# Rotated query columns of all heads as two blocks ahead of attention, plain columns by pairs of heads

## The chip, the cores and the metric

The kernel runs on one core of a Trainium2 chip. The metric is the device time of one execution in microseconds, the median of several runs.

## The reference

The program is an encoder of two layers, 1024 positions by 1024 columns, in float32. What the change touches is the query side of the attention branch: a query of a head has 64 plain columns and 32 that are rotated by the position (two halves of 16, x1 and x2).

```python
def apply_rope(x, cos, sin):
    half = x.shape[-1] // 2
    x1, x2 = x[..., :half], x[..., half:]
    return jnp.concatenate([x1 * cos - x2 * sin, x1 * sin + x2 * cos], axis=-1)

def mla_branch(cq, ckv, kr, cos, sin, q_norm_g, w_uq, kv_norm_g, w_ukv, w_oa):
    q = (rmsnorm(cq, q_norm_g) @ w_uq).reshape(B, S, 8, 96)         # 64 plain, 32 rotated
    q_rope = apply_rope(q[..., 64:], cos[:, :, None], sin[:, :, None])
    kv = (rmsnorm(ckv, kv_norm_g) @ w_ukv).reshape(B, S, 8, 128)
    k_nope, v = kv[..., :64], kv[..., 64:]
    k_rope = apply_rope(kr, cos, sin)                               # one for all heads
    q = concatenate([q[..., :64], q_rope]) * 96 ** -0.5
    k = concatenate([k_nope, broadcast(k_rope)])
    ... softmax(q @ k.T) @ v for each head ...
    return o @ w_oa

def reference(...):
    for l in range(2):
        h = rmsnorm(x) * (1 + sc1) + sh1
        cq, ckv, kr, pu, cx, cb, cc, gl = split(h @ w_in[l])
        ya, yb, yc = mla_branch(...), pool_branch(...), conv_branch(...)
        gates = sigmoid(gl + b_gate[l])
        x = x + g1 * ((gates[0] * ya + gates[1] * yb + gates[2] * yc) @ w_out[l])
        x = x + g2 * ec_moe(h2, ...)
    return rmsnorm(x)
```

## The kernel before

Every product of float32 operands is made from a high and a low part: `split` (L115) writes the high part by a cast on ScalarE and the low part by a subtraction on VectorE, and `mm3` (L325) issues three matmuls for each 512 columns: high by high, high by low, low by high. Activations lie with the columns on the partitions and the 1024 positions along the row.

A layer first makes the branches' inputs. From L651 the low-rank query input `cq` (three groups of 128 rows, `cqhi`, `cqlo`) and the key and value input `ckhi`, `cklo` are made and normed. Then a loop of four weight blocks, `for dp in range(4)` (L754), makes the eight parts d = 0 to 7 of the first gate: `proj` (48 matmuls of 128x512 into one `ps` accumulator of 128x1024), a sigmoid on ScalarE (L769), a store of the gate and, on the way, a load, a multiplication (L766) and a store of a part of `w_out`. The weight blocks come through a ring of two buffers each for `raw`, `whi` and `wlo`; three `ps` accumulators rotate. I call this the gate loop.

Attention follows (L779). `v_tile` makes the values. `k_pair` (L805) makes the plain key rows of two heads in one go, 12 matmuls, and splits the query weights of the pair into `qw`: seven pieces, as columns are put in another order: for an even head the 64 plain columns, the 32 rotated ones and once more the 32 with the halves exchanged; for an odd head the other way round. Both heads of a pair so have 128 rows. `q_head` (L826) makes the 128 query rows of one head in two `pa` banks of 512 positions, nine matmuls each; VectorE multiplies a bank by a table (`tab_e` for even heads, `tab_o` for odd: ones in the plain rows, cosine and signed sine in the others) and the result is split into `qs[h]`. The key rows that stand against the rotated ones hold the rotated key `krope` twice (`rope_part`), once for either product, so the scores' sum over 128 rows adds the two.

The work of attention is a list of 64 units (head h, tile t of 128 positions): `scores` (6 matmuls, maximum, exponential, scaling), `trans` (8 transposes through two `pa` banks, split) and, for every second unit, `av` (16 matmul steps with two forms). Scores run two units ahead (LA = 2). Into this order the blocks are put by hand: `q_head(h + 1)` at t = 2 of an even head, `k_pair` of the next pair at t = 1 of an odd head, and `q_head(h + 1)` at t = 4 of an odd head. There are four `pa` banks and two `ps` accumulators in attention. All instructions of an engine run in the order in which they are issued; loads go by SP's queue, stores and a few loads by POOL's.

Of the kernel before, what the change touches and what calls it, by code (L numbers as in the profile page):

```python
# [18 lines left out]
S = 1024  # L19
# [35 lines left out]
def encoder(ctx, tc, x, c, positions, w_mod, b_mod, norm1_g, w_in, b_gate, q_norm_g, w_uq, kv_norm_g,  # L55
# [31 lines left out]
    def ps2():  # L87
        return pstate["pool"].tile([128, 1024], F32, name="ps", tag="ps", bufs=pstate["n"][0])
# [25 lines left out]
    def split(hi, lo, src):  # L114
        return ACT.copy(hi, src), DVE.tensor_sub(lo, src, f(hi))  # L115
# [19 lines left out]
    tabd = dram.tile([2, 128, S], F32, name="tabd")  # L135
# [12 lines left out]
    for q in range(4):  # L148
        for r in range(4):
            DVE.tensor_copy(krsel[32 * r:32 * r + 32, 32 * q:32 * q + 32], ident[0:32, 0:32])  # L150
# [112 lines left out]
    def rope_tables(ip):  # L263
# [29 lines left out]
        one = ip.tile([128, S], F32, name="one", tag="ra")  # L293
        ACT.activation(sn, sn, AF.Copy, scale=sgn)
        DVE.memset(one, 1.0)
        for (i, r, src) in ((0, 0, one), (0, 64, cs), (0, 96, sn), (1, 0, cs), (1, 32, sn), (1, 64, one)):
            n = 64 if src is one else 32
            SP.dma_start(tabd[i, r:r + n, :], src[r:r + n, :])
# [28 lines left out]
    for l in range(DEPTH):  # L327
# [327 lines left out]
        tab_e = Cq.tile([128, S], F32, name="tab_e")  # L655
        SP.dma_start(tab_e, tabd[0])
        tab_o = Cq.tile([128, S], F32, name="tab_o")
        SP.dma_start(tab_o, tabd[1])
        kwhi = Cq.tile([128, 2, 512], F32R, name="kwhi")
        kwlo = Cq.tile([128, 2, 512], F32R, name="kwlo")  # L660
        with pool("cqt", side="left") as cp:
            def low(w, c0):
                p = ps2()
                proj(p, w, c0)
                return p
# [47 lines left out]
            DVE.tensor_mul(kt_[0:64], p[0:64], tab_o[0:64])  # L713
            DVE.tensor_mul(kt_[64:128], p[64:128], tab_e[64:128])
# [12 lines left out]
            split(kwhi, kwlo, raw.rearrange("p k h c -> p k (h c)"))  # L727
            def prepare(pp):
# [24 lines left out]
            for dp in range(4):  # L753
                wg = block()  # L754
                for d in (2 * dp, 2 * dp + 1):
# [22 lines left out]
        with pool("att", side="right") as ap:  # L778
# [27 lines left out]
            def k_pair(hp):  # L806
# [3 lines left out]
                qw[hp] = [ap.tile([128, 3, 256], F32R, name=f"qw{i}", bufs=1) for i in range(2)]  # L810
# [9 lines left out]
                for (d0, s0, n) in ((0, 0, 96), (96, 80, 16), (112, 64, 16),  # L820
                                    (128, 160, 32), (160, 176, 16), (176, 160, 16), (192, 96, 64)):
                    split(qw[hp][0][:, :, d0:d0 + n], qw[hp][1][:, :, d0:d0 + n], raw[:, :, s0:s0 + n])

            def q_head(h):
                w = qw[h // 2]
                i = h % 2  # L826
                cc = slice(128 * i, 128 * i + 128)
                tab = tab_e if i == 0 else tab_o
# [68 lines left out]
            q_head(0)  # L897
# [6 lines left out]
            for n, (h, t) in enumerate(units):  # L904
# [12 lines left out]
                if h % 2 == 0 and t == 2:  # L917
                    q_head(h + 1)
# [643 lines left out]
```

## Time and profile before

| what | value |
|---|---|
| median of 3 runs (lowest, highest) | 3388.4 us (3385.19, 3395.47) |
| the profiled execution: its time, its span | 3388.24 us, 3386.5 us |
| TensorE busy, share of the span | 3201.4 us, 95% |
| VectorE busy | 2442.3 us, 72% |
| ScalarE busy | 1857.7 us, 55% |
| mean granted clock of TensorE | 0.971 |

The profile is one execution of the program. A time in it is in microseconds from the start of the span; its lines name the kernel's line, the engine, the operation and the tiles as out<-in. PE is TensorE, DVE VectorE, ACT ScalarE, POOL GpSimd and SP the engine whose queue issues the loads. In layer 1 the gate loop ends at about 620 us, and attention runs to about 890; layer 2 repeats both some 1670 us later. An idle time in brackets stands with what ended it.

### The profile page before, as it was taken

The numbers are of one execution on the slowest core, as the hardware profiler recorded it, in microseconds if no ns is written. First come the engines' busy times: TensorE is split into PE (matmuls) and PEld (weight loads), VectorE is DVE, ScalarE is ACT, GpSimd is POOL, SyncE is SP. The second block draws the span as 40 slices with busy tenths as digits, with TensorE's granted clock in tenths as the row PEclk, the third lists the DMA queues.
The fourth block names the chain that finished last, engine by engine and source line by source line (L and its number), as shares of the span: only waits on it lengthen the run. The fifth ranks groups of instructions, "written<-read, shape, count | busy, mean of one in ns | idle before, by whom it ended". The sixth has DMA issues, their size and how long they took to land.

```text
span 3386.5 us, 43057 instructions
## 1 busy us (share of the span) xinstructions
PE 3201.4 (95%) x16593; PEld 2672.0 (79%) x16593; DVE 2442.3 (72%) x3730; ACT 1857.7 (55%) x2535; POOL 384.2 (11%) x364
## 2 busy tenths in 40 slices
PE   6999999999978899999989999999998969999996
PEld 5888887788877688888778888887887968888875
DVE  5556525599848899999864355338997489999997
ACT  5111213588634788887631121317885448888876
POOL 2001001000034001001020000010001330001010
PEclk8999999999988899999999999999999979999998
DMA  6346334000445899999622444340015559999994
GB/s 222 118 151 203 125 114 162 33 17 13 138 177 217 301 390 381 388 391 373 254 60 81 132 157 149 103 156 17 20 38 171 199 193 358 387 389 380 389 378 176
DMA packets 283374, 686.00 MB, mean 203 GB/s; under 512 B 24935, under 2 KB 139841, under 8 KB 283169
## 3 DMA queue, kind: packets, MB, share of 16 engines
q1 hardware_dynamic: 247008, 563.13, 44.8%
q0 software_dynamic: 33856, 111.74, 10.4%
q10 hardware_dynamic: 2304, 8.39, 0.7%
q8 instruction: 130, 2.13, 0.3%
q14 instruction: 76, 0.61, 0.1%
HBM read 607.63 MB, written 75.55 MB: 202 GB/s over the span
## 4 chain that ended last, share of the span: by engine, by line
PE 77%; DVE 12%; ACT 4%; DMA 3%; issue 2%; POOL 1%; SPq 0%; POOLq 0%; DVEq 0%; ACTq 0%
PE ps L325 62%; PE pa L1142 4%; DVE wlo L115 3%; PE pa L325 2%; DVE mx L846 2%; PE pa L864 2%; PE ps L1351 1%; PE pa L872 1%; PE pa L874 1%; DMA gh<-gate 1%; ACT pexp L851 1%; ACT whi L115 1%; DVE af L1065 1%; PE pa L1183 1%; DVE top L1063 1%
## 5 line engine op out<-in xcount | busy, mean ns | idle before, releaser
L115 DVE TENSOR_TENSOR wlo<-rg,whi 128x1024 fp32r<-128x1024 f32 x768 | 899.5, 1219 | 99.2 <-ACT whi L115 95.7
L115 ACT CAST whi<-rg 128x1024 fp32r<-128x1024 f32 x768 | 763.8, 1048 | 181.0 <-PE ps L325 181.0
L325 PE MATMUL ps<-whi,T 128*128 128x512 f32 x3072 | 841.8, 393 | 4.0 <-ACT T L115 2.2
L325 PEld LDWEIGHTS ps<-whi,T 128*128 128x128 f32 x3072 | 574.8, 189 | 126.4 <-ACT T L115 3.1
L325 PE MATMUL ps<-wlo,T 128*128 128x512 f32 x1536 | 489.1, 400 | 5.0 <-DVE wlo L115 3.0
L325 PE MATMUL ps<-hhi,whi 128*128 128x512 f32 x1376 | 427.4, 392 | 0.0
L325 PE MATMUL ps<-hlo,whi 128*128 128x512 f32 x1376 | 423.9, 389 | 0.0
L325 PE MATMUL ps<-hhi,wlo 128*128 128x512 f32 x1376 | 423.8, 389 | 0.0
L325 PEld LDWEIGHTS ps<-wlo,T 128*128 128x128 f32 x1536 | 281.3, 189 | 74.3 <-DVE wlo L115 19.0
L115 ACT CAST whi<-raw 128x2048 fp32r<-128x2048 f32 (+2 forms) x59 | 101.1, 1713 | 417.1 <-PE ps L325 360.8
L325 PEld LDWEIGHTS ps<-hhi,whi 128*128 128x128 f32 x1376 | 256.9, 188 | 58.9 <-issue 4.2
L325 PEld LDWEIGHTS ps<-hlo,whi 128*128 128x128 f32 x1376 | 258.3, 188 | 54.1
L325 PEld LDWEIGHTS ps<-hhi,wlo 128*128 128x128 f32 x1376 | 258.3, 188 | 54.0
L1142 PE MATMUL pa<-rg 128*128 128x256 f32 x768 | 191.4, 304 | 28.1 <-DVE rg L115 13.4
L115 DVE TENSOR_TENSOR wlo<-raw,whi 128x2048 fp32r<-128x2048 f32 (+2 forms) x59 | 120.9, 2050 | 98.5 <-ACT whi L115 98.5
L1142 PEld LDWEIGHTS pa<-rg 128*128 128x128 f32 x768 | 148.9, 206 | 31.3 <-DVE rg L115 14.5
L325 PE MATMUL ps<-khi,raw 128*128 128x512 f32 x512 | 166.5, 406 | 7.2 <-ACT pexp L851 5.7
L115 DVE TENSOR_TENSOR wlo<-pa,whi 128x512 fp32r<-128x512 f32 x256 | 169.3, 680 | 1.3 <-ACT whi L115 1.1
L1444 POOL DMA_INDIRECT xres<-y,idx x30 | 72.5, 2416 | 779.4 <-DVE y L1443 779.4
L851 ACT ACTIVATE pexp<-ps,nm 128x1024 f32<-128x1024 f32 x128 | 143.1, 1118 | 30.4 <-DVE nm L848 27.9
L846 DVE TENSOR_REDUCE mx<-ps 128x1 f32<-128x1024 f32 x128 | 155.0, 1212 | 5.4 <-PE ps L325 4.5
L115 ACT CAST whi<-pa 128x512 fp32r<-128x512 f32 x256 | 139.6, 588 | 7.6 <-PE pa L864 6.5
(409 smaller groups left out, 4899.6 us busy)
## 6 DMA issues: line engine op xcount, KB each, us to landing
rg<-in_w_gate_dram SPq DMA_DIRECT2D x128, 1024.0 KB, 8.9
rg<-in_w_up_dram SPq DMA_DIRECT2D x128, 1024.0 KB, 6.9
rg<-in_w_down_dram SPq DMA_DIRECT2D x128, 1024.0 KB, 7.8
raw<-in_w_mod_dram SPq DMA_DIRECT2D x48, 1024.0 KB, 5.4
raw<-in_w_in_dram SPq DMA_DIRECT2D x43, 1024.0 KB, 5.2
part<-pr POOLq DMA_DIRECT2D x32, 512.0 KB, 4.9
pr<-part POOLq DMA_DIRECT2D x16, 512.0 KB, 4.3
sq<-in_w_out_dram POOLq DMA_DIRECT2D x16, 512.0 KB, 4.4
```

The lines of the kernel that those rows point to most:

```text
L115: return ACT.copy(hi, src), DVE.tensor_sub(lo, src, f(hi))
L325: PE.matmul(dst[:, s], a, b[:, s], start=start and i == 0, stop=stop and i == 2)
L846: DVE.reduce_max(mx, p, axis=AX.X)
L851: ACT.activation(e, p, AF.Exp, bias=nm, scale=SCALE, accum_out=sm)
L864: PE.transpose(p[:, 128 * k:128 * k + 128], e[:, o:o + 128], ident)
L872: PE.matmul(po[:, o:o + 256], vt[:, k, h, :], phi[:, k, :], start=(k == 0), stop=False, skip_group_check=True)
L874: PE.matmul(po[0:64, o:o + 256], vt[:, k, h, 0:64], plo[:, k, :], start=False, stop=(k == 7), skip_group_check=True)
L1063: DVE.max(v[:, 15 - r, :], a)
L1065: DVE.match_replace(a, v[:, 15 - r, :], a, -1.0)
L1142: PE.matmul(p[q // 2][:, 256 * (q % 2):256 * (q % 2) + 256], a, wos[q][b][:, k, :], skip_group_check=True, start=(k == 0 and i == 0 and q ...
L1183: PE.matmul(pls[t][:, :E], hT[:, 128 * k:128 * k + 128], wra[:, kk, :], start=(kk == 0), stop=(kk == 7))
L1444: POOL.indirect_dma_start(out=xres[l], in_=y, in_offset=None, compute_op=OP.add, out_offset=bass.IndirectOffsetOnAxis(ap=idx[e][:, 0:1], a ...
```

## The change

`q_head` goes, and with it the tables `tab_e`, `tab_o` and the doubled columns. In its place:

- `q_rope`, once a layer, in the gate loop behind the gate's part d = 3 (its weights are asked for at d = 2). The rotated columns of all eight heads are two blocks of 128 columns: x1 of all heads, x2 of all heads. Each is 18 matmuls of 128x512 into one `ps` accumulator. Cosine and sine are loaded; four multiplications, a subtraction and an addition of 128x1024 rotate all heads at once; both results are split, and high and low parts stored to memory (`qrd`) in four stores of 512 KB.
- `q_pair`, four times a layer: the 64 plain columns of two heads stand together in one block of 128, 18 matmuls into two `pa` banks. Each bank is split by halves, 64 rows to the one head's query tile and 64 to the other's. The rotated rows come by two loads of 256 KB a head from `qrd`, on SP's queue. The second copy meets key rows that are zero now (`krsel`, which spreads the rotated key over the rows, is filled for two of four groups).
- The query weights of a pair are split in one piece. Every third head's queries have a tile of their own (`q3`).
- `q_pair` stands at t = 4 of an odd head and ahead of the first unit; at the even heads nothing is put in.
- The tables in memory are cosine, sine, and one for the key.

```diff
+            def q_rope(raw):
+                w = [W.tile([128, 3, 2, 8, 16], F32R, name=n_, tag=n_) for n_ in ("whi", "wlo")]
+                for i in range(2):
+                    split(w[0][:, :, i], w[1][:, :, i], raw[:, :, :, 16 * i:16 * i + 16])
...
+                for i in range(2):
+                    p = ps2()
+                    for k in range(3):
+                        mm3(p, w[0][:, k, i], w[1][:, k, i], cqhi[:, k], cqlo[:, k], k == 0, k == 2)
+                    ps.append(p)
...
+                SP.dma_start(cos, tabd[0])
+                SP.dma_start(sin, tabd[1])
...
+                for i, (a, b) in enumerate(((cos, sin), (sin, cos))):
+                    DVE.tensor_mul(r[2 * i], ps[0], a)
+                    DVE.tensor_mul(r[1], ps[1], b)
+                    (DVE.tensor_add if i else DVE.tensor_sub)(r[2 * i], r[2 * i], r[1])
+                    lo = r[2 * i].bitcast(F32R)
+                    split(hi, lo, r[2 * i])
+                    POOL.dma_start(qrd[l][i, :, 0, :], f(hi))
+                    POOL.dma_start(qrd[l][i, :, 1, :], r[2 * i])
...
                     POOL.dma_start(gate0d[l][d], g)
+                    if d == 2:
+                        rope_raw = q_rope_load()
+                    if d == 3:
+                        q_rope(rope_raw)
...
-                for (d0, s0, n) in ((0, 0, 96), (96, 80, 16), (112, 64, 16),
-                                    (128, 160, 32), (160, 176, 16), (176, 160, 16), (192, 96, 64)):
-                    split(qw[hp][0][:, :, d0:d0 + n], qw[hp][1][:, :, d0:d0 + n], raw[:, :, s0:s0 + n])
-
-            def q_head(h):
...
-                qs[h] = W.tile([128, 2, S], F32R, name="raw", tag="raw", bufs=2)
+                split(qw[hp][0], qw[hp][1], raw.rearrange("p k (i c) -> p k i c", c=96)[:, :, :, 0:64])
+
+            def q_pair(hp):
+
+                w = [a.rearrange("p k i c -> p k (i c)") for a in qw[hp]]
+                for h in (2 * hp, 2 * hp + 1):
+                    if h % 3 == 2:
+                        qs[h] = ap.tile([128, 2, S], F32R, name="q3", bufs=1)
+                    else:
+                        qs[h] = W.tile([128, 2, S], F32R, name="raw", tag="raw", bufs=2)
+                    r = 64 * (1 - h % 2)
+                    for o in (0, 32):
+                        SP.dma_start(f(qs[h][r + o:r + o + 32]), qrd[l][:, 16 * h:16 * h + 16])
                 for q in range(2):
                     s_ = slice(512 * q, 512 * q + 512)
                     p = ps1()
                     for k in range(3):
-                        mm3(p, w[0][:, k, cc], w[1][:, k, cc], cqhi[:, k, s_], cqlo[:, k, s_], k == 0, k == 2)
-                    qf = ap.tile([128, 512], F32, name="pexp", tag="pexp", bufs=3)
-                    DVE.tensor_mul(qf, p, tab[:, s_])
-                    split(qs[h][:, 0, s_], qs[h][:, 1, s_], qf)
+                        mm3(p, w[0][:, k], w[1][:, k], cqhi[:, k, s_], cqlo[:, k, s_], k == 0, k == 2)
+                    for i in range(2):
+                        r = slice(64 * i, 64 * i + 64)
+                        split(qs[2 * hp + i][r, 0, s_], qs[2 * hp + i][r, 1, s_], p[r])
...
-                    q_head(h + 1)
                     if h + 1 == H - 1:
...
                     if t == 4:
-                        q_head(h + 1)
+                        q_pair(h // 2 + 1)
```

Where the rope block stands on TensorE, in the middle of the gate loop of layer 1 (`hhi`, `hlo` are the gate's input, `cqhi`, `cqlo` the query input; `wrs` is a small step behind one of the gate's parts). Before, behind the sixth part:

```order
L325 MATMUL ps<-hlo,whi 128x512 x2
L325 MATMUL ps<-hhi,wlo 128x512 x2
L750 MATMUL pa<-wrs,ones 128x16
L325 MATMUL ps<-hhi,whi 128x512 x2
L325 MATMUL ps<-hlo,whi 128x512 x2
```

Now, behind the fourth:

```order
L328 MATMUL ps<-hhi,whi 128x512 x2
L328 MATMUL ps<-hlo,whi 128x512 x2
L328 MATMUL ps<-hhi,wlo 128x512 x2
L784 MATMUL pa<-wrs,ones 128x16
L328 MATMUL ps<-cqhi,whi 128x512 x2
L328 MATMUL ps<-cqlo,whi 128x512 x2
L328 MATMUL ps<-cqhi,wlo 128x512 x2
```

The small step has moved two parts forward, and the 18 groups of the rope block (36 matmuls) stand behind it, ahead of the fifth part.

ScalarE in the same place, with the semaphores that each row waits for (`cf<-ps,vec` is a sigmoid of the gate, `whi<-raw` a cast of weights). Before:

```order
L769 ACTIVATE cf<-ps,vec 128x1024 [waits PE_49]
L115 CAST ckhi<-cf 128x1024 [waits DVE_49] x2
L115 CAST whi<-raw 128x2048 [waits DMAHW6_49,PE_49]
L769 ACTIVATE cf<-ps,vec 128x1024 [waits DMASW5_49,PE_49,Activation_49]
L769 ACTIVATE cf<-ps,vec 128x1024 [waits DVE_49,PE_49]
L115 CAST whi<-raw 128x2048 [waits DMAHW7_49,PE_49]
```

Now:

```order
L115 CAST whi<-raw 128x2048 [waits DMAHW5_49,PE_49]
L803 ACTIVATE cf<-ps,vec 128x1024 [waits DMASW5_49,PE_49,Activation_49]
L803 ACTIVATE cf<-ps,vec 128x1024 [waits DVE_49,PE_49]
L115 CAST whi<-raw 128x3x128 [waits DMAHW6_49,DMAHW7_49,DMAHW0_49,PE_49]
L115 CAST whi<-raw 128x3x128
L803 ACTIVATE cf<-ps,vec 128x1024 [waits DVE_49,PE_49]
L115 CAST whi<-raw 128x2048 [waits DMAHW1_49,DVE_49,PE_49]
L115 CAST rhi<-cf 128x1024 [waits DMASW2_49,DMASW6_49,DMASW1_49,DVE_49]
L115 CAST rhi<-cf 128x1024 [waits DMASW3_49,DVE_49,Activation_49]
L803 ACTIVATE cf<-ps,vec 128x1024 [waits DMASW7_49,PE_49]
```

Two casts of rope weights have come in ahead of the next weight block's cast, and wait for TensorE; the casts of the rotated rows (`rhi`) stand between a weight block and the next sigmoid.

VectorE in attention, in the second half of head 1, where the queries of head 2 were made and those of heads 2 and 3 are made now (`wlo<-pa` is the split behind a transpose, `mx` and `nm` belong to the scores). Before:

```order
L884 TENSOR_TENSOR op<-pa,otmp 64x512
L836 TENSOR_TENSOR pexp<-pa,tab_e 128x512
L115 TENSOR_TENSOR raw<-pexp,raw 128x512
L836 TENSOR_TENSOR pexp<-pa,tab_e 128x512
L846 TENSOR_REDUCE mx<-ps 128x1
L115 TENSOR_TENSOR raw<-pexp,raw 128x512
L848 TENSOR_SCALAR nm<-mx 128x1
```

Now:

```order
L925 TENSOR_TENSOR op<-pa,otmp 64x512
L115 TENSOR_TENSOR q_4922<-pa,q_4922 64x512
L115 TENSOR_TENSOR raw<-pa,raw 64x512
L115 TENSOR_TENSOR qw_5497<-uq,qw_5496 128x384
L115 TENSOR_TENSOR q_4922<-pa,q_4922 64x512
L887 TENSOR_REDUCE mx<-ps 128x1
L115 TENSOR_TENSOR raw<-pa,raw 64x512
L889 TENSOR_SCALAR nm<-mx 128x1
L115 TENSOR_TENSOR wlo<-pa,whi 128x4x128 x2
```

Two multiplications and two subtractions of 128 rows have become four subtractions of 64 rows, which read the accumulator `pa` themselves; the subtraction of query weights in one piece stands between them. The like rows of the even heads, four of them with seven pieces of query weights, have nothing in their place.

## Rows read from the trace of the kernel before

**Rows 1.** The page, parts 1 and 4: busy time by engine, chain by engine.

```profile
PE 3201.4 (95%) x16593; PEld 2672.0 (79%) x16593; DVE 2442.3 (72%) x3730; ACT 1857.7 (55%) x2535; POOL 384.2 (11%) x364
...
PE 77%; DVE 12%; ACT 4%; DMA 3%; issue 2%; POOL 1%; SPq 0%; POOLq 0%; DVEq 0%; ACTq 0%
```

**Rows 2.** Table by stretches: gate loop, a pair of heads (columns: first line).

```profile
core 0: us, PE busy (x) PEld busy (x) DVE busy (x) ACT busy (x) POOL busy (x), PEclk, DMA share, GB/s
560.00:620.00 60.00, 60.00 (x267) 49.73 (x266) 12.35 (x14) 8.34 (x7) 9.57 (x18) 1.00 0.47 167
665.88:729.48 63.60, 63.16 (x402) 55.09 (x400) 59.38 (x120) 53.61 (x99) 0.53 (x1) 1.00 0.04 14
```

**Rows 3.** Timeline of TensorE, gate loop: start, duration (us), line, operation.

```profile
571.77 0.62 PE L325 MATMUL ps<-hlo,whi 128*128 128x512 f32 x2
...
576.75 0.61 PE L325 MATMUL ps<-hhi,whi 128*128 128x512 f32 x2
...
581.74 0.62 PE L325 MATMUL ps<-hhi,wlo 128*128 128x512 f32 x2
```

**Rows 4.** Timeline of TensorE in attention, a query block and two units.

```profile
761.14 0.39 PE L325 MATMUL pa<-cqhi,qw 128*128 128x512 f32 x1
...
765.27 0.61 PE L325 MATMUL ps<-khi,raw 128*128 128x512 f32 x2
...
771.63 0.63 PE L325 MATMUL ps<-khi,raw 128*128 128x512 f32 x2
...
778.03 0.63 PE L325 MATMUL ps<-khi,raw 128*128 128x512 f32 x2
```

**Rows 5.** VectorE's groups in one pair: busy us, mean ns, idle before.

```profile
L115 DVE TENSOR_TENSOR wlo<-pa,whi 128x512 fp32r<-128x512 f32 x33 | 21.8, 681 | 0.0
...
L836 DVE TENSOR_TENSOR pexp<-pa,tab_e 128x512 f32<-128x512 f32 x2 | 1.4, 692 | 0.1
...
L115 DVE TENSOR_TENSOR qw<-uq,qw 128x48 fp32r<-128x48 f32 x4 | 0.6, 200 | 0.0
L115 DVE TENSOR_TENSOR qw<-uq,qw 128x288 fp32r<-128x288 f32 x1 | 0.4, 448 | 0.0
L115 DVE TENSOR_TENSOR qw<-uq,qw 128x192 fp32r<-128x192 f32 x1 | 0.4, 351 | 0.0
L115 DVE TENSOR_TENSOR qw<-uq,qw 128x96 fp32r<-128x96 f32 x1 | 0.3, 251 | 0.0
```

**Rows 6.** Timelines: VectorE and ScalarE in the gate loop, TensorE's wait after it.

```profile
571.73 1.23 DVE L766 TENSOR_TENSOR sq<-sq,rk 128x1024 f32<-128x1024 f32 x1 [6.45 <-DMA sq<-in_w_out_dram]
...
576.50 1.91 ACT L115 CAST whi<-raw 128x2048 fp32r<-128x2048 f32 x1 [9.31 <-PE ps L325]
...
629.06 0.50 PE L325 MATMUL pa<-cqhi,qw 128*128 128x512 f32 x1 [1.39 <-ACT qw L115]
```

**Rows 7.** Timeline of the first key block: ScalarE and VectorE on one half.

```profile
626.35 0.58 ACT L115 CAST khi<-pa 64x512 fp32r<-64x512 f32 x1
...
627.18 0.67 DVE L115 TENSOR_TENSOR klo<-pa,khi 64x512 fp32r<-64x512 f32 x1
```

**Rows 8.** DMA issues from 540 to 640 us: count, KB each, us to landing.

```profile
sq<-in_w_out_dram POOLq DMA_DIRECT2D x8, 512.0 KB, 4.4
...
woutd<-sq POOLq DMA_DIRECT2D x8, 512.0 KB, 3.4
```

**Rows 9.** Table by stretches: around a gap of TensorE in either layer.

```profile
648.00:652.00 4.00, 2.17 (x14) 1.67 (x14) 4.00 (x8) 2.77 (x5) 0.00 (x0) 1.00 0.00 0
652.00:656.00 4.00, 4.00 (x16) 3.30 (x17) 2.93 (x6) 2.45 (x4) 0.00 (x0) 0.57 0.00 0
2318.00:2322.00 4.00, 2.17 (x15) 1.66 (x13) 4.00 (x8) 2.78 (x6) 0.00 (x0) 1.00 0.00 0
2322.00:2326.00 4.00, 4.00 (x29) 3.69 (x30) 4.00 (x11) 3.51 (x6) 0.00 (x0) 1.00 0.00 0
```

More of the change, by code (lines that the diff above doesn't have):

```diff
@@ L134, in encoder @@
     gate0d = [dram.tile([8, 128, S], F32, name=f"gate0{l}") for l in range(DEPTH)]
-    tabd = dram.tile([2, 128, S], F32, name="tabd")
+    tabd = dram.tile([3, 128, S], F32, name="tabd")
+    qrd = [dram.tile([2, 128, 2, S], F32, name=f"qrd{l}") for l in range(DEPTH)]
     woutd = [dram.tile([8, 128, D], F32, name=f"woutd{l}") for l in range(DEPTH)]
@@ L147, in encoder @@
     krsel = consts.tile([128, 128], F32, name="krsel")
-    for q in range(4):
+    DVE.memset(krsel, 0.0)
+    for q in (0, 2):
         for r in range(4):
@@ L292, in rope_tables @@
         DVE.tensor_scalar(sgn, sgn, 0.125, -1.0, op0=OP.mult, op1=OP.add)
[L293 to L298, printed above, removed]
+        turned = ip.tile([128, S], F32, name="turned", tag="ra")
+        ACT.activation(turned, sn, AF.Copy, scale=sgn)
+        SP.dma_start(tabd[0], cs)
+        SP.dma_start(tabd[1], sn)
+        for (r, src) in ((0, cs), (32, turned), (64, cs), (96, turned)):
+            SP.dma_start(tabd[2, r:r + 32, :], src[r:r + 32, :])
     def rms_scale(src, n, scr):
@@ L654, in encoder @@
         krope = Cq.tile([128, S], F32, name="krope")
[L655 to L658, printed above, removed]
         kwhi = Cq.tile([128, 2, 512], F32R, name="kwhi")
@@ L661, in encoder @@
         with pool("cqt", side="left") as cp:
+            tab_k = cp.tile([128, S], F32, name="tab_k")
+            SP.dma_start(tab_k, tabd[2])
             def low(w, c0):
@@ L712, in encoder @@
             kt_ = cp.tile([128, S], F32, name="cf", tag="cf", bufs=3)
-            DVE.tensor_mul(kt_[0:64], p[0:64], tab_o[0:64])
-            DVE.tensor_mul(kt_[64:128], p[64:128], tab_e[64:128])
+            DVE.tensor_mul(kt_, p, tab_k)
             def k_rope():
@@ L727, in encoder, with q_rope_load @@
             split(kwhi, kwlo, raw.rearrange("p k h c -> p k (h c)"))
+            def q_rope_load():
+                raw = W.tile([128, 3, 8, 32], F32, name="raw", tag="raw")
+                for k in range(3):
+                    SP.dma_start(raw[:, k], w_uq[l][128 * k:128 * k + 128, :].rearrange("p (h c) -> p h c", c=96)[:, :, 64:96])
+                return raw
+            def q_rope(raw):
+                w = [W.tile([128, 3, 2, 8, 16], F32R, name=n_, tag=n_) for n_ in ("whi", "wlo")]
+                for i in range(2):
+                    split(w[0][:, :, i], w[1][:, :, i], raw[:, :, :, 16 * i:16 * i + 16])
+                w = [a.rearrange("p k i h c -> p k i (h c)") for a in w]
+                ps = []
+                for i in range(2):
+                    p = ps2()
+                    for k in range(3):
+                        mm3(p, w[0][:, k, i], w[1][:, k, i], cqhi[:, k], cqlo[:, k], k == 0, k == 2)
+                    ps.append(p)
+                cos, sin = (cp.tile([128, S], F32, name="sq", tag=n_, bufs=1) for n_ in ("sq", "rb"))
+                SP.dma_start(cos, tabd[0])
+                SP.dma_start(sin, tabd[1])
+                r = [cp.tile([128, S], F32, name="cf", tag="cf", bufs=3) for _ in range(3)]
+                hi = cp.tile([128, S], F32R, name="rhi")
+                for i, (a, b) in enumerate(((cos, sin), (sin, cos))):
[6 more added lines that the diff above has]
+                    POOL.dma_start(qrd[l][i, :, 1, :], r[2 * i])
             def prepare(pp):
@@ L809, in k_pair @@
                 SP.dma_start(raw, w_uq[l][:, 192 * hp:192 * hp + 192].rearrange("(k p) f -> p k f", p=128))
-                qw[hp] = [ap.tile([128, 3, 256], F32R, name=f"qw{i}", bufs=1) for i in range(2)]
+                qw[hp] = [ap.tile([128, 3, 2, 64], F32R, name=f"qw{i}", bufs=1) for i in range(2)]
                 cc = slice(128 * hp, 128 * hp + 128)
@@ L896, in encoder @@
             k_pair(0)
-            q_head(0)
+            q_pair(0)
             for u in units[:LA]:
```

4 lines of the change are left out of this document (removed).

## Prediction

> **What bounds the kernel now.** I read the page first: its list of busy times and its chain of work that ended last [rows 1]. TensorE is busy 95% of the span, and 77% of the chain is its own work, so an edit is worth what it takes from TensorE or makes it wait. A whole-span average hides stages, so next I read the table by stretches for the two places that the change touches [rows 2]. In the gate loop (560 to 620 us) TensorE is busy all 60.00 us while VectorE has 12.35 and ScalarE 8.34: there a matmul costs its own length, and everything else has room. In attention one pair of heads (665.88 to 729.48) takes 63.60 us, TensorE 63.16, VectorE 59.38, ScalarE 53.61; that is TensorE's bound too, but with VectorE only 4 us behind. The granted clock is 1.00 (its upper level, 2.4 GHz) in both stretches.
>
> Third, the timelines of TensorE, for the price of one matmul at each place. In the gate loop 44 matmuls of 128x512 lie between the starts 571.77 and 581.74 [rows 3]: 9.97 / 44 = 0.2266 us each. In attention a query block's 18 matmuls run from 761.14 to the next scores at 765.27 [rows 4]: 4.13 us. Two units (a unit is one 128-row tile of one head: scores, transposes, half an a·v) run from 771.63 to 778.03: 6.40 us. A pair has 16 units, two query blocks and one key block of 12 matmuls: 8 × 6.40 + 2 × 4.13 + 12 × 0.2266 = 62.2 of the 63.60 us. So some 1.4 us a pair is left for waits, and a block that vanishes should shorten the pair by its whole length.
>
> **What goes.** Query blocks: 8 a layer become 4, so 4 × 2 layers × 4.13 = 33.0 us of TensorE. VectorE loses, per pair, four multiplications with the tables (0.692 us) and seven small subtractions of query weights (0.4 + 0.6 + 0.4 + 0.3) [rows 5] for which one of 128x384 comes; between the pieces of 288 (448 ns) and of 512 columns (681 ns) I estimate it at 0.55 us. That is 2.8 + 1.15 = 3.9 us, so VectorE goes from 59.4 to 55.5 in a pair whose TensorE time goes to 63.60 − 4.13 = 59.5. The ratio of the two stays at 0.93: VectorE does not become the bound, and is no less close to it.
>
> **What comes.** The rope block in the gate loop: 36 matmuls a layer, 36 × 0.2266 = 8.16 us, 16.3 for both layers. Its VectorE work (six operations of 128x1024, 1.23 us each by the 1.23 us of such a multiplication [rows 6], two subtractions for the split, two small ones for weights: about 11 us) lies in a stretch where VectorE is free four fifths of the time, and is free as long as that stays so. The next gate blocks need the accumulators it reads: three pairs of banks rotate there and a gate block takes 48 × 0.2266 = 10.9 us, longer than the two multiplications that read each, so I cost that at nothing.
>
> **The wait ahead of it.** In the order of ScalarE the casts of the rope weights stand directly behind the fourth gate block, and they write the buffer that this block's last matmuls read. Before, at such a place, the cast began at 576.50 [rows 6] while the next block's matmuls began at 576.75 [rows 3]: it starts some 0.25 us ahead of the end, once the last reader of the high part is done. A cast of 512 columns took 0.58 us [rows 7]; by columns 384 would take 0.44, by length alone 0.58, so my estimate is 0.5 us, and TensorE can go on another hand-off later: a wait of about 0.5 us a layer. The ends are 0 (cast hidden behind the two matmuls with the low part) and 1.39 us, which TensorE waited for query weights at 629.06 [rows 6]. I take 0.5, nearest to the row at the same place: 1.0 us for both.
>
> **DMAs and queues.** Per layer there are four more stores of 512 KB on the POOL queue and, on the SP queue, 16 loads of 256 KB, three of rope weights and one table more than before. Stores of 512 KB landed in 3.4 us and loads of 512 KB in 4.4 [rows 8]; DMA was busy 0.47 in the gate stretch and 0.04 in attention [rows 2]. Behind the rope block stand four gate blocks, 43.5 us, ahead of attention's first read; the four stores, with the three transfers of one gate block among them, are some 25 us. In attention a load waits only for the last reader of its tile, at least seven units (22 us) ahead of its use. Behind them on SP stands nothing due sooner than the next pair's weights, and on POOL the gate stores that nobody reads until the merge. I cost all this at nothing; with that cover gone, one late load is its 4.4 us.
>
> **The new query block.** Two heads share one bank now. ScalarE's cast of one half, VectorE's subtraction, then the second half's cast and subtraction go strictly one behind the other, since each row waits for the other engine's. Before, a bank was free after one multiplication of 0.69 us. At the key block, which has the same half-bank form, the cast started at 626.35, the subtraction at 627.18, and it lasted 0.67 [rows 7]: 1.50 us for one half, 3.0 for a bank. The first bank's chain ends 0.94 us after the block's last matmul (3.0 less the 2.06 that the second bank's nine matmuls take), the second's 3.0 later, at 3.94. Scores use other banks, 1.36 us for six matmuls; one bank of the four is free for the first transposes; the first of the two comes free before the second transposes, and the second (3.94 us) before the next unit's (3.20 + 1.36). Counted by this TensorE needn't wait. Other work in the two queues will stretch it: I allow 0.7 us, half of the 1.4 us a pair loses now, and the block that vanished gives the same back. Net 0, between −0.7 (nothing waits) and +3.9 us a pair (TensorE stands until the last half is out).
>
> By the Trainium skill, PSUM — Partial Sum Buffer, "PSUM bank collisions raise a hardware error", two engines need keeping apart only in the same bank and the same quadrant of 32 partitions. The two halves are in different quadrants, so the alternation is stricter than the page asks, and with both in parallel a bank would be free sooner than my 3.0 us; the order of the changed kernel keeps it, so the sum stays as it is. By the page alone a bank would need 0.58 + 1.50 = 2.1 us, and (b) below would be 2.1 × 8 = 17, about 3389 us; no row here shows two engines in one bank at once.
>
> **The sum**, against the profiled execution of 3388.24 us (the median of the three runs is 3388.4, so nothing shifts): 3388.24 − 33.0 + 16.3 + 1.0 + 0 = **3372.5 us**, 0.46% less. About 0.3% is what a measurement of this kernel can tell from no change: 3378.1 and 3398.4.
>
> **Rivals.** (a) *Each query block costs one half-bank chain.* Place: second transposes behind the block wait 1.5 us, because casts and subtractions of other units stand between the halves. For it: VectorE's 59.38 of 63.60 leaves it little slack; against: the count above. 8 × 1.5 = 12: 3384.5 us. It leaves the forecast's side from 0.7 us a block, (3378.1 − 3372.5) / 8.
>
> (b) *Slower: TensorE stands until the last half is out.* 3.94 × 8 = 31.5: 3404.0 us. It decides from 15.7 / 8 = 1.96 us a pair, and is measurably slower from 3.2. For it: the alternation and two heads in one chain; against: scores don't need these banks, and one bank is free.
>
> (c) *The gap ahead of the rope block lowers the clock.* After 1.83 us without a matmul (TensorE busy 2.17 of 4 us, 648 to 652) the granted clock was 0.57 in the next 4 us; after an equal gap in the second layer (2318 to 2322) it stayed at 1.00 [rows 9]. If the rope block ran wholly at the lower level, its 36 matmuls would cost twice as much, 16.3 us more for both layers: 3388.8 us, no change. Against it: my wait is 0.5 us, not 1.83, and one of two longer gaps left no mark. The Trainium skill, TensorE: Matmul & The Clock Gate, "What's actually happening", says that the gate halves the clock after idleness and restores it with activity; by that rule, a gap of this kind either costs nothing or a short stretch, and these rows agree and show both outcomes.
>
> (d) *It doesn't do what it says*: rotated rows arrive late, or the scheduler's order turns the saved blocks into waits for exponentials. The pair keeps its 63.6 us: TensorE's saving goes and the rope block stays, 3388.24 + 17.3 = 3405.5 in full, or about no change with half of it. I see no row for it.
>
> (e) *Better*: the waits around the vanished block go as well, 0.7 × 8 = 5.6: 3366.9 us.
>
> **How the numbers follow.** Forecast (3371 to 3377, by the hand-off's bounds and small waits) 0.52; (e) 0.07; (a) 0.17, of which 0.03 under 0.7 us a block; (c) 0.09; (b) 0.10; (d) 0.05, with 0.01 of it slower. Faster: 0.52 + 0.07 + 0.03 = 0.62. Within 0.3%: 0.14 + 0.09 + 0.04 = 0.27. Slower: 0.10 + 0.01 = 0.11. The range goes from 3365 (just under (e)) to 3389 (just over (c)), leaving out (b), part of (d) and some of (e).
>
> **What would show it.** In the trace after: a pair of heads at 59.5 us with TensorE some 59 busy (right), or 61 and more with idle time ahead of transposes, put down to VectorE's subtraction on a half bank (a, b). The gate loop longer by 8.2 + 0.5 us a layer, with one idle gap of about half a microsecond, put down to ScalarE's cast, ahead of the first rope matmul; a granted clock below 1.00 behind it means (c). An idle gap put down to a load of query rows means (d). I'm wrong if the pair shortens by less than 3 us, or the rope block costs more than 10 us a layer.

## The result and the profile after

The changed kernel takes 3369.15 us (median of 7 runs, 3365.76 to 3375.81) against 3388.4 us (median of 7, 3383.96 to 3395.47); the ratio is 0.9948, 95% interval 0.9939 to 0.9958. That is 19.2 us less, where 15.7 were forecast (3372.5 us). The profiled execution took 3369.31 us, its span is 3367.5.

The page after, parts 1 and 4, as [rows 1]:

```profile
PE 3182.2 (94%) x16521; PEld 2656.2 (79%) x16521; DVE 2432.3 (72%) x3660; ACT 1853.9 (55%) x2495; POOL 388.7 (12%) x372
...
PE 78%; DVE 11%; issue 3%; ACT 3%; DMA 3%; POOL 1%; SPq 0%; POOLq 0%; ACTq 0%; DVEq 0%
```

TensorE's busy time fell by 19.2 us and VectorE's by 10.0. The table by stretches, as [rows 2] (gate loop, the rope block alone, the second and third pair of heads):

```profile
560.00:620.00 60.00, 59.98 (x266) 49.59 (x265) 22.44 (x24) 11.28 (x11) 11.30 (x22) 1.00 0.69 236
577.34:585.50 8.16, 8.16 (x36) 6.75 (x37) 2.43 (x4) 1.48 (x3) 0.53 (x1) 1.00 0.70 195
689.78:749.21 59.43, 58.99 (x386) 51.82 (x384) 55.85 (x111) 52.83 (x94) 0.53 (x1) 1.00 0.09 32
749.21:808.61 59.40, 58.96 (x385) 51.81 (x383) 56.13 (x110) 52.52 (x94) 0.53 (x1) 1.00 0.08 32
```

The rope block takes 8.16 us for its 36 matmuls. A pair of heads takes 59.43 and 59.40 us, 4.2 less than before; VectorE is busy 55.85 of them. Both are as forecast. What was not forecast stands between the two places. TensorE's timeline, first query block of layer 1 and of layer 2:

```profile
641.91 0.80 PE L328 MATMUL pa<-cqhi,qw 128*128 128x512 f32 x1 [6.94 <-ACT qw L115]
...
2303.35 0.79 PE L328 MATMUL pa<-cqhi,qw 128*128 128x512 f32 x1 [5.12 <-ACT qw L115]
```

The idle time in brackets is 6.94 and 5.12 us; before it was 1.39 us there [rows 6] (1.58 in layer 2). To see where time came and went I cut each layer at the starts of four matmuls that both kernels have: the first value matmul, the second key block, the fourth key block, and the first matmul of the merge behind attention. Differences after less before, in us:

| stretch | forecast | layer 1 | layer 2 |
|---|---|---|---|
| up to the first value matmul (gate loop with the rope block; for layer 2 from the first layer's merge) | +8.7 | +7.2 | +7.2 |
| first value matmul to second key block (entry of attention) | −4.1 | −1.4 | −1.4 |
| second to fourth key block (two pairs) | −8.3 | −8.4 | −8.4 |
| fourth key block to the merge | −4.1 | −4.0 | −5.1 |
| sum | −7.9 | −6.6 | −7.7 |

That is −14.3 of the span's −19.0. The other 4.7 us lie behind layer 2's merge, in code that the change doesn't touch: 827.96 us before, 823.26 after. In the eleven experiments below the same stretch took between 824.7 and 827.4 us, in kernels of either kind, so executions differ there by some 3 us of themselves; the two values compared here lie just outside this range, one at either end. Whether a part of the 4.7 belongs to the change stays open.

### The profile page after: what moved, and what is told of

It reads as the page before. It is cut to its first block, busy times and chain, and to the rows that moved or that the text cites. A ratio compares the mean times of both kernels' runs of the same rounds, so it can differ in the third digit from the quotient of the medians.

```text
span 3367.5 us, 42973 instructions
## 1 busy us (share of the span) xinstructions
PE 3182.2 (94%) x16521; PEld 2656.2 (79%) x16521; DVE 2432.3 (72%) x3660; ACT 1853.9 (55%) x2495; POOL 388.7 (12%) x372
## 4 chain that ended last, share of the span: by engine, by line
PE 78%; DVE 11%; issue 3%; ACT 3%; DMA 3%; POOL 1%; SPq 0%; POOLq 0%; ACTq 0%; DVEq 0%
PE ps L328 63%; PE pa L1182 4%; PE pa L905 3%; DVE wlo L115 3%; PE pa L913 2%; PE pa L915 2%; PE pa L328 1%; PE ps L1391 1%; DMA gh<-gate 1%; ACT whi L115 1%; DVE af L1105 1%; DVE gh L1014 1%; DVE top L1103 1%; DVE mx L887 1%; PE ps L493 1%
## 5 line engine op out<-in xcount | busy, mean ns | idle before, releaser
L115 ACT CAST whi<-raw 128x2048 fp32r<-128x2048 f32 (+3 forms) x63 | 103.0, 1637 | 429.9 <-PE ps L328 382.9
L115 DVE TENSOR_TENSOR wlo<-raw,whi 128x2048 fp32r<-128x2048 f32 (+3 forms) x63 | 123.0, 1955 | 97.0 <-ACT whi L115 96.9
L232 DVE SCALAR_TENSOR_TENSOR macc<-raw,csil,macc 128x256 f32<-128x256 f32 x280 | 135.1, 484 | 8.4
```

Of the source, the lines that this page charges most:

```text
L232: DVE.scalar_tensor_tensor(acc, raw[:, k], csil[:, k:k + 1], acc, op0=OP.mult, op1=OP.add)
```

## The entry of attention: where a forecast gain went

Why does TensorE stand there? The timelines of SP, POOL and ScalarE in the changed kernel, layer 1:

```profile
629.36 1.25 SPq L870 DMA_DIRECT2D q<-qrd  x2
...
630.83 0.53 POOL L804 DMA_DIRECT2D gate<-cf  x1 [10.40 <-ACT cf L803]
...
639.30 1.07 ACT L115 CAST vt<-pa 128x512 fp32r<-128x512 f32 x2 [7.69 <-issue]
640.26 1.07 ACT L115 CAST khi<-pa 64x512 fp32r<-64x512 f32 x2
641.35 0.51 ACT L115 CAST qw<-uq 128x384 fp32r<-128x384 f32 x1
...
2300.73 1.07 ACT L115 CAST vt<-pa 128x512 fp32r<-128x512 f32 x2 [5.87 <-DMA gate<-cf]
```

Read from below: the cast of the first query weights (641.35) stands on ScalarE behind the keys' cast and the first value split (639.30). That split waited 7.69 us; the profile names no releaser in layer 1, but in layer 2 (the last row) it names the store of the last gate. The value tile lies where the last gates' tiles were, so it has to wait for their stores. The last store was issued at 630.83, 8.5 us before the split started and 1.5 us behind two loads of rotated rows (629.36) on the other queue. The DMA lists from 600 to 645 us (count, KB each, median us to landing), of the kernel before and of the changed one, and the changed one's table by stretches read:

```profile
gate<-cf POOLq DMA_DIRECT2D x3, 512.0 KB, 2.9
...
gate<-cf POOLq DMA_DIRECT2D x4, 512.0 KB, 8.8
...
625.00:630.00 5.00, 5.00 (x24) 4.14 (x23) 0.00 (x0) 0.58 (x1) 0.00 (x0) 1.00 0.13 55
635.00:640.00 5.00, 0.00 (x0) 0.00 (x0) 0.08 (x1) 0.70 (x2) 0.00 (x0) 0.88 0.13 53
640.00:645.00 5.00, 3.09 (x7) 2.49 (x8) 4.54 (x7) 4.90 (x9) 0.00 (x0) 0.50 0.28 96
...
2300.00:2305.00 5.00, 1.65 (x4) 1.36 (x5) 3.65 (x6) 4.22 (x7) 0.00 (x0) 0.61 0.13 54
2305.00:2310.00 5.00, 5.00 (x17) 3.93 (x17) 2.87 (x5) 3.39 (x6) 0.00 (x0) 0.71 0.30 99
```

A gate store that landed in 2.9 us now takes 8.8. While only loads of rotated rows run (625 to 630, 635 to 640) the DMA share is 0.13, the share of two of sixteen engines, and 53 to 55 GB/s move: 256 KB then take almost 5 us. If a store is spread over all sixteen engines, it ends only when its part on those two does; the traces don't show single engines, so this is argued. My theory A: the loads run on two engines, the last gate store waits behind them there, the value split waits for the store, the query weights for the split, TensorE for the weights. Rivals: theory B, that the volume of transfers or ScalarE's own order makes the wait, whatever the loads' form; and, for the sum as a whole, that the gain in a pair came from VectorE's and ScalarE's lost work and not from TensorE's.

The Trainium skill, DMA: Bandwidth & Descriptors, "Rules for kernel authors", says that a transfer whose outermost dimension has a size c below 16 stays on at most c DMA engines. The loads read from two blocks (x1 and x2) of 16 rows, so c is 2; the share of 0.13 agrees.

The clock shows a second price. After the idle time the granted clock was 0.50 in layer 1 (640 to 645), the lower of its two levels, and 0.61 and 0.71 in layer 2. The 18 matmuls of the query block and the 12 of two scores cost 6.84 us at the upper level (18 × 0.229 + 12 × 0.2266); they took 8.7 and 9.1 us, from 641.91 to the next value matmul at 650.60 and from 2303.35 to 2312.43.

## The experiments

Each run was taken beside runs of the kernel before, whose median was 3386.2 to 3386.8 us in these sets and 3388.4 us in the first. So a difference of medians of two sets is uncertain by some 2 us from this alone; for smaller differences I go by the stretches of the trace.

**The loads spread wide.** Theory A's first link.

```diff
                     for o in (0, 32):
-                        SP.dma_start(f(qs[h][r + o:r + o + 32]), qrd[l][:, 16 * h:16 * h + 16])
+                        for i in range(2):
+                            SP.dma_start(f(qs[h][r + o + 16 * i:r + o + 16 * i + 16]), qrd[l][i, 16 * h:16 * h + 16])
```

> The changed kernel with each head's rotated rows loaded by four loads of 128 KB (16 rows of 8 KB each) in place of two of 256 KB (two times 16 rows); same bytes, same queue, same places. Theory A: in the changed kernel the loads of 256 KB keep only two of the sixteen DMA engines busy (DMA share 0.13 while they run), the last gate store is held up on those two, the first value split on ScalarE waits for that store, and TensorE stands 6.94 and 5.12 us ahead of the first query block with its clock down after it. Spread wider, the wait falls to 1 to 2 us in each layer and the granted clock stays near 1.00 behind it: 12 to 16 us less, about 3355 us. Theory B: the number of DMA engines is not what matters (the volume of transfers or ScalarE's own order is): the two waits stay, 3369 us as the changed kernel.

Measured: 3361.97 us (ratio to before 0.9928, 0.9914 to 0.9941). TensorE's first query block in both layers, then the gate stores and the loads in the DMA list from 585 to 645 us, then the table by stretches:

```profile
637.67 0.50 PE L328 MATMUL pa<-cqhi,qw 128*128 128x512 f32 x1 [3.08 <-ACT qw L115]
...
2294.56 0.79 PE L328 MATMUL pa<-cqhi,qw 128*128 128x512 f32 x1 [2.86 <-ACT qw L115]
...
gate<-cf POOLq DMA_DIRECT2D x4, 512.0 KB, 5.8
...
raw<-qrd SPq DMA_DIRECT2D x8, 128.0 KB, 5.2
...
q<-qrd SPq DMA_DIRECT2D x4, 128.0 KB, 4.2
...
600.00:605.00 5.00, 5.00 (x24) 4.14 (x23) 0.00 (x0) 0.00 (x0) 1.08 (x3) 1.00 1.01 389
625.00:630.00 5.00, 5.00 (x24) 4.05 (x22) 0.00 (x0) 0.97 (x1) 0.00 (x0) 1.00 0.05 8
...
2295.00:2300.00 5.00, 5.00 (x13) 3.83 (x13) 3.00 (x5) 3.95 (x6) 0.00 (x0) 0.50 0.43 111
```

The idle time fell from 6.94 and 5.12 to 3.08 and 2.86 us. The same bytes now go at full rate (share 1.01 and 389 GB/s where they run beside the stores), and those of heads 0 and 1 are over before the last gate block ends (0.05 from 625 to 630). The value split started 4.6 us behind the last gate store's issue (630.43 to 635.05), not 8.5. The entry took 4.0 us less in layer 1, but only 1.6 in layer 2: there the clock fell after the shorter gap too (0.50 from 2295 to 2300, last row), and the 30 matmuls of the query block and two scores took 9.72 us (2294.56 to 2304.28) where they took 9.08 in the changed kernel. Theory A holds for the loads' form; my number was too high, since a wait of 3 us stays and the clock didn't stay up: 7.2 us by the medians, and 5.6 when each kernel is set against the kernel before of its own set, which is also the sum of the two entries; not 12 to 16.

The form isn't all of the stores' delay: with the same bytes in wide loads a gate store still lands in 5.8 us (first row of the DMA list), between the 2.9 before and the 8.8 of the changed kernel, so the volume of transfers, theory B's part, has a share in it. Nor did the edit change the form alone: two of head 2's four loads went out behind the store, at 639.08, so that half as many of head 2's bytes stood ahead of it. The next run takes all of them from there.

**Head 2's loads behind the store.** The order of the two transfers.

```diff
-                        SP.dma_start(f(qs[h][r + o:r + o + 32]), qrd[l][:, 16 * h:16 * h + 16])
+                        (POOL if h == 2 else SP).dma_start(f(qs[h][r + o:r + o + 32]), qrd[l][:, 16 * h:16 * h + 16])
```

> The changed kernel with the two loads for head 2 alone issued on POOL's queue, so that they stand behind the last gate store and not ahead of it; all other loads as they are. Theory A (the store is held up by the loads issued just ahead of it): the store lands 3 to 4 us after its issue, the wait of TensorE falls to about 2 us in each layer, 8 to 14 us less, about 3358 us. If the loads of heads 0 and 1 still held the store up, the wait would stay at 5 us or more. Theory B (volume or order on ScalarE): 3369 us.

Measured: 3365.37 us (0.9935, 0.9922 to 0.9949). Timeline of TensorE:

```profile
637.52 0.80 PE L328 MATMUL pa<-cqhi,qw 128*128 128x512 f32 x1 [4.22 <-ACT qw L115]
...
2296.77 0.79 PE L328 MATMUL pa<-cqhi,qw 128*128 128x512 f32 x1 [4.51 <-ACT qw L115]
```

The idle time is 4.22 and 4.51 us: less than in the changed kernel, more than the 2 us expected, and in layer 2 hardly less. The entry took 2.9 us less in layer 1 and in layer 2 as long as before the edit (59.15 us for 59.17). The value split started 5.8 and 6.0 us behind the store's issue, so the store wasn't out 3 to 4 us behind it, as I had expected. Part of my 2 us was too little from the start: even with wide loads the split started 4.6 us behind, with 3.08 us of idle TensorE. What this run has above the idle time with wide loads is 1.1 and 1.7 us; heads 0 and 1 still load in the old form, and head 2's loads now run beside the store. It speaks for A weakly, and in layer 1 alone. It also speaks against fewer bytes ahead of the store as the explanation of what wide loads gained: with none of head 2's ahead of it the wait was longer, not shorter.

**Without the rope block's matmuls**, on narrow loads and on wide ones. What does the block cost?

```diff
-                    p = ps2()
-                    for k in range(3):
-                        mm3(p, w[0][:, k, i], w[1][:, k, i], cqhi[:, k], cqlo[:, k], k == 0, k == 2)
-                    ps.append(p)
...
+                ps = [f(cqhi[:, 0]), f(cqhi[:, 1])]
```

> The changed kernel without the 36 matmuls and the weights of the rope block: the rotation is fed from two groups of the query input, so the rotated columns are not the reference's; all multiplications, splits, stores and loads stay. By the prediction's sum the block is 8.16 us of TensorE in each layer and no wait: 16.3 us less, 3353 us. If the gate loop were set by its transfers or by VectorE now that the rotation stands in it, the time would stay nearer to 3369 us.

> The changed kernel with the loads spread wide (four of 128 KB a head) and without the 36 matmuls and weights of the rope block (rotation fed from the query input, so the rotated columns are not the reference's). Beside the kernel with wide loads alone (3361.97 us) it prices the block where no transfer is late. Theory A (the block costs its 36 matmuls, 8.16 us a layer; the run without it on narrow loads was slower only because the loads then came last): 16 us less, 3346 us, TensorE's wait ahead of the first query block 3 to 6 us. Theory B (transfers behind the rotation are the bound whatever their width): the wait grows by about 8 us a layer and the time stays at 3360 us or more.

Measured on narrow loads: 3380.73 us (0.9983, 0.9973 to 0.9992), 11.6 us more than the changed kernel with 72 matmuls fewer, where I had expected 3353 or, at worst, 3369. On wide loads: 3348.44 us (0.9887, 0.9872 to 0.9902), 13.5 less than with the block. The waits ahead of the first query block, narrow and then wide, with ScalarE's value split of the narrow one:

```profile
644.35 0.80 PE L328 MATMUL pa<-cqhi,qw 128*128 128x512 f32 x1 [16.62 <-ACT qw L115]
...
2311.02 0.80 PE L328 MATMUL pa<-cqhi,qw 128*128 128x512 f32 x1 [20.72 <-ACT qw L115]
...
641.74 1.07 ACT L115 CAST vt<-pa 128x512 fp32r<-128x512 f32 x2 [18.73 <-DMA q<-qrd]
```

```profile
622.45 0.50 PE L328 MATMUL pa<-whi,ckhi 128*128 128x512 f32 x1 [1.21 <-ACT cf L794]
...
631.63 0.50 PE L328 MATMUL pa<-cqhi,qw 128*128 128x512 f32 x1 [3.44 <-ACT qw L115]
...
2281.19 0.80 PE L328 MATMUL pa<-cqhi,qw 128*128 128x512 f32 x1 [4.00 <-ACT qw L115]
```

With narrow loads the time that TensorE no longer spends on the block comes back as waiting, and more: 16.62 and 20.72 us, and the value split waited 18.73 us until the transfers were out. The entry is set by the end of the slow transfers, and the four gate blocks behind the rotation are what hides them; in the changed kernel this cover was too short. The missing 8.16 us of cover, added to the old waits, would make 15.1 and 13.3 us; the 1.5 and 7.4 us above that stay unexplained. With wide loads the block is worth what its matmuls say: 16.3, less 2.4 for a wait that its absence brings back (1.21 us ahead of the first value matmul in each layer, first row of the second fence) and 1.5 for a longer wait ahead of the query block (3.44 and 4.00, not 3.08 and 2.86), leaves 12.4; 13.5 were measured.

**Query matmuls put back**, 18 at each even head, read by nobody.

```diff
                 if h % 2 == 0 and t == 2:
+                    w = [a.rearrange("p k i c -> p k (i c)") for a in qw[h // 2]]
+                    for q in range(2):
+                        s_ = slice(512 * q, 512 * q + 512)
+                        p = ps1()
+                        for k in range(3):
+                            mm3(p, w[0][:, k], w[1][:, k], cqhi[:, k, s_], cqlo[:, k, s_], k == 0, k == 2)
```

> The changed kernel with 18 matmuls put back at the third unit of every even head, into two banks that nobody reads: four such blocks a layer, no work for another engine. If TensorE's own time sets a pair of heads, as the prediction's sum has it, each costs 4.13 us: 33 us more, about 3402 us, and a pair goes back from 59.4 to 63.5 us. If the pair's gain came from VectorE's and ScalarE's work that went with the old blocks, the matmuls fit into waits and the time stays under 3385 us.

Measured: 3401.93 us (1.0042, 1.0028 to 1.0055), 32.8 more than the changed kernel by the medians; the touched stretches of the two traces differ by 31.3. Its second pair in the table by stretches:

```profile
694.25:757.52 63.27, 62.94 (x404) 55.23 (x402) 56.19 (x110) 52.77 (x94) 0.53 (x1) 1.00 0.08 30
```

A pair takes 63.27 us, nearly what it took before (63.60), though VectorE has only 56.19 us of work in it. So 3.9 of the 4.2 us that a pair gained come back with the matmuls alone: the pair's gain is TensorE's time, and the rival falls.

**The first key block ahead of the values**, meant to get the query weights' cast out from behind the value split. On narrow loads, on wide ones, and in the kernel before:

```diff
+            k_pair(0)
             for t in range(2):
                 v_tile(t)
-            k_pair(0)
             q_pair(0)
```

> The changed kernel, loads narrow as they are, with the first key block put ahead of the first two value tiles, and so the casts of keys and query weights ahead of the value split that waits for the last gate store. Theory A (TensorE stands because the casts of query weights are queued on ScalarE behind that split): TensorE works through keys, values and the first query block meanwhile, the idle ahead of the first query block falls from 6.9 and 5.1 to under 1 us, some 2 us may come back ahead of the first scores: 8 to 14 us less, about 3358 us. Theory B (query weights or keys come late themselves, by the same slow transfers): the wait stays, 3369 us.

> The changed kernel with wide loads and with the first key block ahead of the first value tiles. Theory A: against wide loads alone (3361.97 us) the remaining 3.1 and 2.9 us ahead of the first query block go, about 3356 us. Theory B (the remaining wait is that of the query weights' own load and cast, as before the change): 3362 us.

> The kernel before with only the first key block put ahead of the first two value tiles. It had 1.25 and 1.39 us (1.25 and 1.58 in the second layer) of idle TensorE at the entry of attention: by theory A at most 2.5 us a layer, 3382 to 3387 us; so the reordering is worth little where no loads are in the way, and what the changed kernel gains by it more than this is the price of its own loads.

Measured: 3372.1 us on narrow loads (ratio to before 0.9955), 3362.04 on wide ones, 3389.51 for the kernel before: no gain anywhere. The timelines of ScalarE and TensorE on narrow loads tell why:

```profile
639.83 1.07 ACT L115 CAST vt<-pa 128x512 fp32r<-128x512 f32 x2 [6.41 <-DMA gate<-cf]
640.92 0.51 ACT L115 CAST qw<-uq 128x384 fp32r<-128x384 f32 x1
...
642.91 0.77 PE L328 MATMUL pa<-cqhi,qw 128*128 128x512 f32 x1 [7.39 <-DVE klo L115]
```

The value split (639.83, waiting 6.41 us for the gate store) still stands ahead of the cast of query weights (640.92): the scheduler kept that order. The first key bank's casts did come ahead of it (632.18), but the second bank's (641.46) stayed behind as well, and the query block's wait (7.39 us) is put down to their subtraction. The edit didn't do what it was to do, and tells nothing against either theory. It does show once more what the split waits for.

**The value tile in another place.** The same link, cut without touching loads or order: keys of heads 2 and 3, needed later, stand where the last gates' tiles were.

```diff
+            late = [[ap.tile([128, S], F32R, name=f"{n_}{i}") for i in (2, 3)] for n_ in ("khi", "klo")]
             vt = ap.tile([128, 8, 8, 128], F32R, name="vt")
-            khi = [ap.tile([128, S], F32R, name=f"khi{i}") for i in range(4)]
-            klo = [ap.tile([128, S], F32R, name=f"klo{i}") for i in range(4)]
+            khi = [ap.tile([128, S], F32R, name=f"khi{i}") for i in range(2)] + late[0]
+            klo = [ap.tile([128, S], F32R, name=f"klo{i}") for i in range(2)] + late[1]
```

> The changed kernel with narrow loads as they are; only the place of tiles in attention's memory is other: the keys of heads 2 and 3 stand where the last gates' tiles were, and the value tile stands behind them, so that the first value split no longer waits for the last gate store. (The run that put the key block first did not do that: on ScalarE the value split still stood ahead of the cast of query weights.) Theory A: the wait ahead of the first query block falls from 6.9 and 5.1 to 1.5 us or less in each layer, the clock stays up: 10 to 14 us less, about 3357 us. Theory B (something else on ScalarE or the query weights' load is late): the wait stays, 3369 us.

> The changed kernel with the loads spread wide and with the value tile moved likewise. Theory A: the 3.1 and 2.9 us that were left with wide loads alone (3361.97 us) fall to some 1.4 us, the price of the first query weights' cast: 3 to 4 us less, about 3358 us, near to the run with the tile moved alone, since both take away the same wait. Theory B: the wait that is left has another cause, 3362 us.

> The kernel before with only the value tile moved. Its value split waited for the last gate store too, but TensorE stood only 1.39 and 1.58 us ahead of the first query block. Theory A: at most 1.5 us a layer, 3384 to 3387 us; a gain of 10 us here would mean that the wait was there before the change and isn't its price.

Measured: 3364.88 us on narrow loads (0.9937, 0.9924 to 0.9951), 3358.32 on wide ones (0.9921, 0.9908 to 0.9935), 3385.88 for the kernel before (1.0, 0.9991 to 1.0009). On narrow loads, layer 1, TensorE's waits and ScalarE's cast of query weights; then the two waits on wide loads:

```profile
637.78 0.50 PE L328 MATMUL pa<-cqhi,qw 128*128 128x512 f32 x1 [2.40 <-ACT qw L115]
...
643.11 0.73 PE L328 MATMUL ps<-khi,raw 128*128 128x512 f32 x2 [0.93 <-ACT raw L115]
...
652.11 0.50 PE L328 MATMUL pa<-whi,ckhi 128*128 128x512 f32 x1 [0.32 <-DVE nm L890]
...
656.25 0.50 PE L328 MATMUL pa<-whi,ckhi 128*128 128x512 f32 x1 [1.13 <-DVE vt L115]
...
632.05 1.24 ACT L115 CAST vt<-pa 128x512 fp32r<-128x512 f32 x2
...
637.22 0.51 ACT L115 CAST qw<-uq 128x384 fp32r<-128x384 f32 x1 [1.22 <-DMA uq<-in_w_uq_dram]
```

```profile
636.33 0.50 PE L328 MATMUL pa<-cqhi,qw 128*128 128x512 f32 x1 [1.20 <-ACT qw L115]
...
2289.13 0.50 PE L328 MATMUL pa<-cqhi,qw 128*128 128x512 f32 x1 [1.20 <-ACT qw L115]
```

On narrow loads the value split starts at 632.05, 2.5 us behind the first value matmul and not 10 us behind it, and the wait of 6.94 us falls to 2.40 (5.12 to 2.77 in layer 2), with no load changed: the split's wait for the store was the link. Only 4.3 us of the expected 10 to 14 arrive by the medians, and that is not clear of the spread (the two ratios' intervals overlap); the waits and stretches carry the reading. What was saved ahead of the query block is partly given back: the query weights wait 1.22 us for their own load, the scores 0.93, and two value tiles 0.32 and 1.13 in layer 1. In layer 2 the clock fell as well (0.66 in the 5 us from 2297.61). From the first value matmul to the second key block the kernel gained 3.0 and 1.0 us. On wide loads nothing is left to give back: 1.20 us ahead of the first query block in both layers, the entry 54.2 us in both (60.6 and 59.2 in the changed kernel). In the kernel before the same move is worth nothing that can be measured. So the longer wait is the price of the change's own transfers, and the version with wide loads and the moved tile beats both kernels: 3358.32 us, 28 less than the 3386.36 us of the kernel before beside it, with a ratio whose interval lies below that of the changed kernel.

## Why the prediction was right, and where it wasn't

The total is right: 3369.15 us against 3372.5, inside the range, faster as forecast. Step by step:

- **TensorE's prices** were right. The rope block took the 8.16 us of the sum. Pairs took 59.4 for a forecast of 59.5, and the four blocks a layer, put back, cost 31.3 to 32.8 us for 33.0.
- **The new query block's net 0** was right. From the second key block to the merge no idle time of TensorE is longer than 0.27 us, but for one of 0.68 near the end of layer 1's attention. The strict turns of ScalarE and VectorE on the half banks cost nothing to see; rivals (a) and (b) fall, and so do (d), whose pair would have kept its 63.6 us, and (e), whose pair would have been 0.7 us shorter.
- **The wait ahead of the rope block** was 0.5 us in the sum and didn't show. TensorE's start of the block and ScalarE's casts:

```profile
576.77 0.93 ACT L115 CAST whi<-raw 128x384 fp32r<-128x384 f32 x2 [9.31 <-PE ps L328]
...
577.03 0.29 PE L784 MATMUL pa<-wrs,ones 128*128 128x16 f32 x2
577.34 0.50 PE L328 MATMUL ps<-cqhi,whi 128*128 128x512 f32 x1
```

  The two casts took 0.93 us, as estimated, but the small step's two matmuls (577.03), which I had left out though the order shows them, cover the rest.
- **A wait that went.** Before, the first value matmul stood 1.25 us for a sigmoid of the gate; in the changed kernel there is none. Both runs without the block's matmuls have it back (1.21 us in each layer), so it hangs on the block. That the block's two more accumulators in the ring of three moved it away is my reading; no run separates it. I hadn't costed this: 2.5 us of gain for both layers.
- **"I cost all this at nothing"** (DMAs and queues) failed. This is the term that was wrong. The loads were in time for their readers, as I had said; but a load can cost by whom it holds up. I took landing times of 128-row transfers [rows 8] for loads whose rows come from two blocks of 16, and the bound that I gave, 4.4 us for one late load, was for the wrong waiter. The price was 5.6 and 3.5 us of longer waits ahead of the query block and some 2 us of clock behind each. At the same place the wait of 1.83 us of [rows 9] is gone, so that the entry as a whole missed its −4.1 by 2.7 us a layer.
- **Rival (c)**, the lower clock after a gap, came true in kind, though not where I looked: the rope block ran at 1.00, the stretch of 5 us in which the first query block began at 0.50 in layer 1 and 0.61 in layer 2, at a price of some 2 us each.

So the two errors have opposite signs, 3.0 us too dear in the gate loop and 5.5 too cheap at the entry, and cancel in part; with another 0.9 us gained behind the fourth key block the sum of the touched stretches is −14.3 for −15.7. That it lies so near is partly luck: the prediction names neither the wait that went nor the one that came. The rest of the measured gain lies in an untouched stretch that varies by some 3 us.

## What to carry to other kernels

When work moves from compute to transfers, look at the form of each new transfer and at whom it may hold up, not only at whether its reader gets it in time: here, beside loads that ran at a DMA share of 0.13, stores on another queue took 8.8 us in place of 2.9, and 5.8 with the same bytes in wide loads. Memory that is reused across stages can tie the next stage's first instruction to the last store of the one before, as the value split was tied to the last gate store; put there what is needed late. And an engine that works in order passes such a wait on to work that has nothing to do with it, as ScalarE did with the cast of query weights.

## What the runs showed of the hardware

Loads of 256 KB with an outer dimension of two ran at a DMA share of 0.13 and 53 to 55 GB/s; the same bytes as loads of 16 rows of 8 KB went beside other transfers at a share of 1.01 and 389 GB/s. After 6.94 us without a matmul the granted clock was 0.50 over the next stretch of 5 us, and after 1.20 us, with wide loads and the moved tile, it was 1.00. In between the same kernel showed both: with wide loads alone it was 0.84 (640 to 645) behind a gap of 3.08 us in layer 1 and 0.50 (2295 to 2300) behind one of 2.86 us in layer 2. The rate of the narrow loads I had not expected; the clock after a gap I had, at another place.
